# A 512-column up-projection, x in 256-column pieces ahead of its weight rows, and an output over two queues

## The chip, the cores and the metric

The kernel runs on one core of a Trainium2 chip. The metric is device time in microseconds (us) for one execution. A core has TensorE (PE) for matrix products, VectorE (DVE), ScalarE (ACT) and GpSimd (POOL) for elementwise work, and SyncE (SP), which here issues nearly all transfers. PE's weight loads have a row of their own (PEld) in the profile. PSUM, where PE accumulates, has 8 banks of 128 partitions x 512 fp32.

## The reference

`x` is 256 x 2048, fp32, one layer. Cut to what matters:

```
h = rmsnorm(x) * norm_mix_g
z = h @ w_in                      # 2048 x 3072: ssm_in | u | v, 1024 columns each
a = glu(S5(ssm_in))               # 64 groups of a complex state space, then a 1024 x 1024 gate
b = SGU(u, v)                     # causal mixing of positions in chunks of 128
x = x + concat(rmsnorm(a), rmsnorm(b)) @ w_out        # 2048 x 2048
x = x + relu(rmsnorm(x) @ w_up)**2 @ w_down           # 2048 x 8192, 8192 x 2048
y = rmsnorm(x)
```

## The kernel before, in words

**Three products for one.** Every fp32 operand is split into a rounded part (hi) and the rest (lo). A product is then hi·xh + hi·xl + lo·xh, with xh and xl the two parts of the activations. All are added up in one PSUM bank.

**The weight stream.** `wparts` brings the weights through in parts of 512 KB: two 128-row tiles of 512 columns (`raw`, one transfer on SP, L152). `split` makes `whi` on ACT (L105) and `wlo` on DVE (L106). There are three buffers of each and four raw ones. The very first part is "fine": two transfers and two splits, one per 128-row tile.

**Two kinds of block.** `block_A` puts weights into the array and streams activations: for each of four 128-column slices `m` and each row tile it does three matmuls of 256 columns (L186, L187, L188: hi·xh, hi·xl, lo·xh), into `banks[m // 2]`, so two banks hold the four slices. `block_B` keeps activations in the array and streams 512 weight columns (L202 to L204).

**The stages.** In order: w_in for z (block_A on two column blocks, then `z_out`, which scales by the row norm `rsB`), sgu v and u, w_out, glu, the other half of w_out, then four rounds (`NF`) of four block_A on w_up and four block_B on w_down. In w_up the activations are `x2T[:, k, 0]` and `x2T[:, k, 1]` (xh and xl, 256 positions each, neighbours in memory). After a w_up block each bank goes through a relu on ACT, and on DVE the square; ACT then writes its hi part `ht[..., 0]` and DVE the lo part. The S5 work runs in the background as generators that `pump` advances after each part. The last w_down block has a bank of its own kind, `accL` (L1048 to L1050): rows 0 to 127 (t = 0) with 512 columns, rows 128 to 255 (t = 1) with two pieces of 256.

**The start.** SP issues gnat (the norm's weights, 16 x 128), the first 256 columns of x (two row halves, `xin`), the first weight tile, and so on; `hooks` is a list of functions that are called one per weight part and issue further pieces of x (512 columns each) and small parameters. PE first does eight dummy matmuls (`pwarm`, L279), then transposes gnat (`pv`, L283) and x (`ptx`, L297). `prep_x(i)` makes two row tiles of `xT`: ACT writes the hi part times gnat (L300), DVE the lo part (L301). `x_stats` (ACT, squares of x) and `x_rstd` give `rsB`.

**The end.** `last_add` adds the last product to `dacc` (L984), squares it with a sum (ACT, L987) into `ss3`, and multiplies by the final norm's weights. `rstd_sqrt` (L268 to L273) computes the inverse root from the sum of the partial sums (L1054); four pieces of 512 columns per t are scaled (L1059, L1061, L1063) and written by SP (L1064).

**What sets the order.** The program is written as one stream; a scheduler orders instructions on each engine, with a planned time for each, within the limits of data and buffers. `tc.issue_after(ins)` adds a limit: what is issued in it stands behind `ins`. `fence` and `behind` use it to keep small matmuls between large ones. `psa` has four PSUM banks for large products, `psx` one and `pss` three for small ones.

Of the kernel before, what the change touches and what calls it, by code (L numbers as in the profile page):

```python
# [49 lines left out]
def hybrid_layer_kernel(  # L50
# [19 lines left out]
    psx = ctx.enter_context(tc.tile_pool(name="psx", bufs=1, space=PSUM))  # L70
    pss_ = ctx.enter_context(tc.tile_pool(name="pss", bufs=3, space=PSUM))
# [13 lines left out]

    def acc(shape, name="acc"):
        return psa.tile(shape, F32, tag="acc", name=nm(name))
# [16 lines left out]
    def split(hi, lo, src):  # L104
        A.activation(hi, src, AF.Copy)  # L105
        V.tensor_sub(lo, src, hi.bitcast(F32))  # L106
# [34 lines left out]
    hooks = []  # L141

    def wparts(w, k0, nk, c0, places=None):

        wp, kd = stream["pool"], stream["kd"]
        for q in range(0, nk, kd):
            raw = wp.tile([P, kd, 512], F32, tag="raw", bufs=stream["raw"], name=nm("raw"))
            r0_ = (k0 + q) * P
            fine = stream.pop("fine", False)
            step = 1 if fine else kd  # L150
            for s in range(0, kd, step):
                nc.sync.dma_start(  # L152
                    raw[:, s : s + step],
                    w[r0_ + s * P : r0_ + (s + step) * P, c0 : c0 + 512].rearrange("(k p) c -> p k c", p=P),
                )
                if fine and s == 0:
                    hooks.pop(0)()
            if hooks:
                hooks.pop(0)()
            for s in range(0, kd, KS):  # L160
                if places:
                    hi, lo = places[(q + s) // KS]
                else:
                    hi = wp.tile([P, KS, 512], F32R, tag="whi", bufs=3, name=nm("whi"))
                    lo = wp.tile([P, KS, 512], F32R, tag="wlo", bufs=3, name=nm("wlo"))
                if fine:
                    for kk in range(KS):
                        split(hi[:, kk], lo[:, kk], raw[:, s + kk])
                else:
                    split(hi, lo, raw[:, s : s + KS])  # L170
                yield q + s, hi, lo

    def block_A(w, k0, nk, c0, act):


        banks = [acc([P, 2, S], "accA") for _ in range(2)]
        for kp0, hi, lo in wparts(w, k0, nk, c0):
            for m in range(4):
                o = banks[m // 2][:, m % 2]
                ms = slice(m * P, m * P + P)  # L180
                for kk in range(KS):
                    kp = kp0 + kk
                    xh, xl = act(kp)
                    first = kp == 0 and m % 2 == 0
                    with behind():
                        T.matmul(o, hi[:, kk, ms], xh, start=first, stop=False, skip_group_check=True)  # L186
                    T.matmul(o, hi[:, kk, ms], xl, start=False, stop=False, skip_group_check=True)  # L187
                    T.matmul(o, lo[:, kk, ms], xh, start=False, stop=(kp == nk - 1), skip_group_check=True)  # L188
                pump(stream["d"] / 4)
        return banks  # L190
# [25 lines left out]
    def load_x(c, n=512):  # L216
        cs_ = slice(c, c + n)
        for t in range(2):
            nc.sync.dma_start(xin[t][:, cs_], x[t * P : (t + 1) * P, cs_])
# [6 lines left out]
    def load_vecs():  # L226
        r0 = 0
        for v in (norm_mlp_g, ong_ssm, ong_sgu, glu_b):
            n = v.shape[1] // P
            nc.sync.dma_start(vnat[r0 : r0 + n, :], v[0].rearrange("(k p) -> k p", p=P))  # L230
            r0 += n

    nc.sync.dma_start(gnat, norm_mix_g[0].rearrange("(k p) -> k p", p=P))
    load_x(0, 256)


# [27 lines left out]
    def rstd_sqrt(dst, ss, scale, n):  # L264

        m = const.tile([P, n], F32, name=nm("rq_m"))
        t1 = const.tile([P, n], F32, name=nm("rq_t"))
        A.activation(dst, ss, AF.Sqrt, scale=scale, bias=eps_c)  # L268
        V.tensor_scalar(m, ss, scale, EPS, ALU.mult, ALU.add)
# [8 lines left out]
    for i in range(WARMUPS):  # L278
        T.matmul(pwarm, onesm, onesm, start=True, stop=True)  # L279

    def prep_vecs(dst, nat, n):
        pv = aux([P, n], "pv")
        T.transpose(pv, nat, ident[:n, :n])  # L283
        V.tensor_copy(dst, pv)
# [6 lines left out]
    def prep_x(i):  # L291

        pt = acc([P, 2, S], "ptx")
        for kk in range(2):
            k = 2 * i + kk
            for t in range(2):
                T.transpose(pt[:, kk, t * P : (t + 1) * P], xin[t][:, k * P : (k + 1) * P], ident)  # L297
        for kk in range(2):
            k = 2 * i + kk
            xins[i] = A.activation(xT[:, k, 0], pt[:, kk], AF.Copy, scale=g_mix[:, k : k + 1])  # L300
            V.scalar_tensor_tensor(  # L301
                xT[:, k, 1], pt[:, kk], g_mix[:, k : k + 1], xT[:, k, 0].bitcast(F32),
                ALU.mult, ALU.subtract,
            )

    xins = {}

    def x_stats(j):
        with tc.issue_after(xins[2 * j + 1].ins):
# [20 lines left out]
    prep_vecs(vecs[:, 0:16], gnat, 16)  # L330
    prep_x(0)
    hook((load_x, 256, 256))
    hook((load_x, 512), (prep_x, 1))
    hook((load_x, 1024), (prep_x, 2), (prep_x, 3))
    hook((load_x, 1536), (x_stats, 0))
    hook((load_small,), (prep_x, 4), (prep_x, 5))
    hook((x_stats, 1))
    hook((prep_x, 6), (prep_x, 7), (x_stats, 2))
    hook((x_stats, 3), (x_rstd,))
# [69 lines left out]
    def gen_scalars():  # L409

        pa = sx([P, 64], "pa")
        T.transpose(pa, anat, ident[:64, :64])
        V.tensor_copy(lam.rearrange("p a q -> p (a q)"), pa)
        ldt = s32("ldt")
        lv = ldt_all.rearrange("p (q g) -> p q g", g=2)
        for g in range(2):
            V.tensor_copy(ldt[g * 64 : (g + 1) * 64, :], lv[g * 64 : (g + 1) * 64, :, g])
# [50 lines left out]
    def gen_ct():  # L468
# [3 lines left out]
        for i, src in enumerate((b_re, b_im, c_re, c_im)):  # L472
            rows_ = bcn[i * 32 : (i + 1) * 32]
            if i < 2:
                nc.sync.dma_start(rows_, src[0].rearrange("(q g) p h -> q (g p h)", g=2))
            else:
                for g in range(2):
                    nc.sync.dma_start(
                        rows_.rearrange("q (c g p) -> q g c p", c=16, g=2)[:, g],
                        src[0].rearrange("(q g) c p -> q g c p", g=2)[:, g],  # L480
                    )
        for e in range(4):
            nc.sync.dma_start(dnat[:, e, :], ssm_d[0].rearrange("(q g) c -> q (g c)", g=2))
# [3 lines left out]
        for which in range(2):  # L487
            rs_ = slice(which * 64, (which + 1) * 64)
            for h2 in range(2):
                pc = sx([P, 8, 2, 32], "pc")  # L490
                for h8 in range(8):
                    T.transpose(
                        pc[:, h8].rearrange("p i q -> p (i q)"),
                        (bn if which == 0 else cn)[:, h2 * 8 + h8], ident[rs_, rs_],
                    )
# [477 lines left out]
    front.close()  # L973
    mp = ctx.enter_context(tc.tile_pool(name="mlp", bufs=1))
# [6 lines left out]
    def last_add(t, c, cw, bank):  # L981
# [56 lines left out]
    for t in range(2):  # L1038
        ts_ = slice(t * P, t * P + P)
        cw = 512 if t == 0 else 256  # L1040
        for c in range(0, 512, cw):
            bank = acc([P, cw], "accL")
            for kp0, hi, lo in parts:
                for kk in range(KS):
# [5 lines left out]
                    T.matmul(bank, xl[:, ts_], wh, start=False, stop=(kp == 15))  # L1050
            last_add(t, c0 + c, cw, bank)
        s3 = const.tile([P, 1], F32, name=nm("s3"))
        r3 = const.tile([P, 1], F32, name=nm("r3"))
        V.tensor_reduce(s3, ss3[:, t], AX.X, ALU.add)  # L1054
        rstd_sqrt(r3, s3, 1.0 / D, 1)
        for n in range(4):
            ns = slice(n * 512, (n + 1) * 512)
            if n == 0:
                V.tensor_scalar(dacc[:, t, ns], dacc[:, t, ns], r3, None, ALU.mult)  # L1059
            elif n == 3:  # L1060
                V.scalar_tensor_tensor(dacc[:, t, ns], dacc[:, t, ns], r3, gfin[:, ns], ALU.mult, ALU.mult)  # L1061
            else:
                A.activation(dacc[:, t, ns], dacc[:, t, ns], AF.Copy, scale=r3)  # L1063
            nc.sync.dma_start(out[t * P : (t + 1) * P, ns], dacc[:, t, ns])  # L1064
# [29 lines left out]
```

## Time and profile before

| what | value |
|---|---|
| three runs | 1062.08, 1059.5, 1062.22 us, median 1062.08 us |
| the profiled execution | 1060.78 us, span 1059.0 us from first to last instruction |
| granted TensorE clock, mean | 0.994 |
| HBM read and written | 189.91 MB and 4.19 MB, 183 GB/s over the span |
| L186, L187, L188 in w_up | 1024 matmuls each |
| weight splits | 337 on ACT (mean 1058 ns), 337 on DVE (mean 1221 ns) |

A row of a group or of the timeline gives start, length, engine, line, operation and tiles ("out<-in"), the shape of output and input, and in square brackets the idle time before it with what ended it. Matmul lengths reach from issue to the modelled end and overlap; their starts tell the pace. In a table of windows the columns are the stretch, its length, busy time (and instructions) of PE, PEld, DVE, ACT and POOL, the granted clock (1.00 is full), the share of the transfer engines, and GB/s. The waits view gives the engine, tile and line that waited, what it waited for, the total, how often, and the longest.

### The profile page before, as it was taken

What the parts mean: (1) busy time and instruction counts of PE and PEld (TensorE: products, weight loads), DVE (VectorE), ACT (ScalarE), POOL (GpSimd) and SP (SyncE); (2) the same over time, 40 slices, a digit from 0 to 9 for tenths busy, and PEclk for the clock granted to TensorE, in tenths of its full rate; (3) what the DMA queues carried; (4) which work ended last, traced back from release to release, by engine and by line L of the source; (5) the groups of instructions that cost most, each with busy time, mean ns of one, the idle gap of its engine ahead of it and who ended that gap; (6) DMA issues with size and microseconds to landing.
All of it is one profiled execution on the core that took longest, in us unless ns stands there. A gap on an engine that the chain in (4) does not pass through costs nothing.

```text
span 1059.0 us, 16980 instructions
## 1 busy us (share of the span) xinstructions
PE 1043.3 (99%) x6881; PEld 951.1 (90%) x6881; DVE 651.3 (62%) x888; ACT 532.1 (50%) x685; POOL 9.5 (1%) x22
## 2 busy tenths in 40 slices
PE   8999999999999999999999999999999999999996
PEld 7997899978989999888999988899998889998886
DVE  6899988686687555544455555545555565555564
ACT  5668676663766444544444443344444434444453
POOL 0101000000000000000000000000000000000000
PEclk8999999999999999999999999999999999999998
DMA  8774554566565666666666666666666666666662
GB/s 239 225 224 133 141 159 105 155 219 196 181 221 178 180 183 184 191 193 192 192 181 182 187 189 196 198 182 183 184 187 191 191 197 182 184 184 187 195 205 97
DMA packets 112047, 195.25 MB, mean 184 GB/s; under 512 B 17753, under 2 KB 21537, under 8 KB 111521
## 3 DMA queue, kind: packets, MB, share of 16 engines
q1 hardware_dynamic: 111712, 194.13, 61.4%
q8 instruction: 54, 0.88, 0.4%
q14 instruction: 25, 0.20, 0.1%
q0 software_dynamic: 256, 0.03, 0.0%
HBM read 189.91 MB, written 4.19 MB: 183 GB/s over the span
## 4 chain that ended last, share of the span: by engine, by line
PE 90%; ACT 3%; DVE 3%; DMA 2%; issue 1%; SPq 0%; ACTq 0%
PE accA L186 14%; PE accA L188 14%; PE accA L187 14%; PE accB L203 14%; PE accB L204 14%; PE accB L202 14%; PE pf L664 1%; DMA raw<-in_w_in_dram 1%; ACT Tp L631 1%; DMA bcn<-in_ssm_c_im_dram 1%; DVE wlo L106 1%; PE py L704 1%; PE accL L1050 1%; PE accL L1049 1%; PE accL L1048 1%
## 5 line engine op out<-in xcount | busy, mean ns | idle before, releaser
L106 DVE TENSOR_TENSOR wlo<-raw,whi 128x1024 fp32r<-128x1024 f32 (+1 forms) x337 | 411.3, 1221 | 372.1 <-ACT whi L105 371.5
L105 ACT ACTIVATE whi<-raw 128x1024 fp32r<-128x1024 f32 (+1 forms) x337 | 355.9, 1058 | 454.9 <-PE accB L204 200.9
L186 PE MATMUL accA<-x2T,whi 128*128 128x256 f32 x1024 | 289.6, 283 | 0.0
L187 PE MATMUL accA<-x2T,whi 128*128 128x256 f32 x1024 | 289.6, 283 | 0.0
L188 PE MATMUL accA<-x2T,wlo 128*128 128x256 f32 x1024 | 289.2, 283 | 0.0
L187 PEld LDWEIGHTS accA<-x2T,whi 128*128 128x128 f32 x1024 | 196.6, 192 | 0.2
L186 PEld LDWEIGHTS accA<-x2T,whi 128*128 128x128 f32 x1024 | 196.6, 192 | 0.2
L188 PEld LDWEIGHTS accA<-x2T,wlo 128*128 128x128 f32 x1024 | 196.3, 192 | 0.0
L203 PE MATMUL accB<-wlo,hT 128*128 128x512 f32 x480 | 186.8, 389 | 0.0
L204 PE MATMUL accB<-whi,hT 128*128 128x512 f32 x480 | 186.7, 389 | 0.0
L202 PE MATMUL accB<-whi,hT 128*128 128x512 f32 x480 | 168.0, 389 | 0.0
L204 PEld LDWEIGHTS accB<-whi,hT 128*128 128x128 f32 x480 | 90.1, 188 | 18.7
L203 PEld LDWEIGHTS accB<-wlo,hT 128*128 128x128 f32 x480 | 90.1, 188 | 18.5
L202 PEld LDWEIGHTS accB<-whi,hT 128*128 128x128 f32 x480 | 90.1, 188 | 18.6
L186 PE MATMUL accA<-xT,whi 128*128 128x256 f32 x256 | 73.5, 294 | 2.4 <-ACT xT L300 2.4
L187 PE MATMUL accA<-xT,whi 128*128 128x256 f32 x256 | 73.8, 291 | 0.0
L188 PE MATMUL accA<-xT,wlo 128*128 128x256 f32 x256 | 72.5, 290 | 0.0
L186 PEld LDWEIGHTS accA<-xT,whi 128*128 128x128 f32 x256 | 49.3, 195 | 3.3 <-ACT xT L300 2.7
L187 PEld LDWEIGHTS accA<-xT,whi 128*128 128x128 f32 x256 | 50.0, 195 | 0.6 <-DVE xT L301 0.3
L188 PEld LDWEIGHTS accA<-xT,wlo 128*128 128x128 f32 x256 | 49.5, 196 | 0.2
L203 PE MATMUL accB<-wlo,xT 128*128 128x512 f32 x64 | 25.8, 403 | 0.0
L204 PE MATMUL accB<-whi,xT 128*128 128x512 f32 x64 | 25.1, 392 | 0.0
(285 smaller groups left out, 1079.9 us busy)
## 6 DMA issues: line engine op xcount, KB each, us to landing
raw<-in_w_up_dram SPq DMA_DIRECT2D x128, 512.0 KB, 3.7
raw<-in_w_down_dram SPq DMA_DIRECT2D x128, 512.0 KB, 4.0
raw<-in_w_in_dram SPq DMA_DIRECT2D x47, 512.0 KB, 4.2
raw<-in_w_out_dram SPq DMA_DIRECT2D x32, 512.0 KB, 4.7
raw<-in_ssm_glu_w_dram SPq DMA_DIRECT2D x8, 512.0 KB, 4.4
x<-in_x_dram SPq DMA_DIRECT2D x2, 1024.0 KB
out_dram<-dacc SPq DMA_DIRECT2D x8, 256.0 KB, 2.6
xin<-in_x_dram SPq DMA_DIRECT2D x6, 256.0 KB, 7.1
```

The lines of the kernel that those rows point to most:

```text
L105: A.activation(hi, src, AF.Copy)
L106: V.tensor_sub(lo, src, hi.bitcast(F32))
L186: T.matmul(o, hi[:, kk, ms], xh, start=first, stop=False, skip_group_check=True)
L187: T.matmul(o, hi[:, kk, ms], xl, start=False, stop=False, skip_group_check=True)
L188: T.matmul(o, lo[:, kk, ms], xh, start=False, stop=(kp == nk - 1), skip_group_check=True)
L202: T.matmul(banks[t], xh[:, ts_], hi[:, kk], start=(kp == 0), stop=False)
L203: T.matmul(banks[t], xh[:, ts_], lo[:, kk], start=False, stop=False)
L204: T.matmul(banks[t], xl[:, ts_], hi[:, kk], start=False, stop=(kp == nk - 1))
L631: A.activation(Tp[e * 32 : (e + 1) * 32, :, g, 3 - e : 4, :], k4[:, :, 0 : e + 1, :], AF.Copy, scale=gmask[:, g : g + 1],)
L664: T.matmul(pfs[r][i][:, q], w1s[r][:, i, q], u2[r][:, q], start=True, stop=True)
L704: last = T.matmul(py[g * 64 : (g + 1) * 64, q], Gp[:, q, g].rearrange("p j c -> p (j c)"), Eg[:, q, g], start=False, stop=True, skip_group ...
L1048: T.matmul(bank, xh[:, ts_], wh, start=(kp == 0), stop=False)
```

## The change

It has three parts.

1. **w_up.** `block_A2` multiplies hi by xh and xl in one matmul of 512 columns (the two lie side by side) and adds lo·xh with one of 256 columns into the second half of the bank, so that hi·xh stands in columns 0 to 255 and hi·xl + lo·xh in 256 to 511. Each slice `m` has a bank of its own, four per block. The pools `psx` and `pss` are closed after the mixed stage, and their four banks become `psm`, with which `psa` takes turns. After a block, ACT copies the second half of each bank to `cr` and DVE adds the first half.
2. **The start.** x comes in pieces of 256 columns, each ahead of the weight part that it meets; the second row half of the first piece is issued by ACT, gnat by GpSimd. The transposes of piece i are done in the middle of the weight part before it (`mids`). There are twice two more `pwarm` matmuls between the first transposes. In the first part of block 0 the order is `which` (0, 2, 1) outside and `m` inside. `x_stats` and `x_rstd` come after block 0. Some parameter loads are tied behind a weight transfer, and groups of small transposes behind large products.
3. **The end.** The partial sums up to the last piece are added before it, and `rstd_sqrt` takes them as its bias beside the last piece's own sum. The output goes out in four (t = 0) or five (t = 1) pieces over SP's and ACT's queues.

```
@@ pools
+    psx = front.enter_context(tc.tile_pool(name="psx", bufs=1, space=PSUM))
+    pss_ = front.enter_context(tc.tile_pool(name="pss", bufs=3, space=PSUM))
...
+    acc_pools = [psa]
     def acc(shape, name="acc"):
-        return psa.tile(shape, F32, tag="acc", name=nm(name))
+        acc_pools.append(acc_pools.pop(0))
+        return acc_pools[-1].tile(shape, F32, tag="acc", name=nm(name))
@@ the up-projection's block
+    def block_A2(w, k0, nk, c0, act):
+        banks = [acc([P, 2, S], "accA") for _ in range(4)]
         for kp0, hi, lo in wparts(w, k0, nk, c0):
             for m in range(4):
-                o = banks[m // 2][:, m % 2]
+                o = banks[m]
                 ms = slice(m * P, m * P + P)
                 for kk in range(KS):
                     kp = kp0 + kk
-                    xh, xl = act(kp)
...
-                    T.matmul(o, hi[:, kk, ms], xl, start=False, stop=False, skip_group_check=True)
-                    T.matmul(o, lo[:, kk, ms], xh, start=False, stop=(kp == nk - 1), skip_group_check=True)
+                    xhl = act(kp)
+                    T.matmul(o, hi[:, kk, ms], xhl, start=(kp == 0), stop=False, skip_group_check=True)
+                    T.matmul(
+                        o[:, 1], lo[:, kk, ms], xhl[:, 0], start=False, stop=(kp == nk - 1),
+                        skip_group_check=True,
+                    )
@@ w_up
     front.close()
+    psm = ctx.enter_context(tc.tile_pool(name="psm", bufs=4, space=PSUM))
+    acc_pools[:] = [psa] * 4 + [psm] * 4
...
-            banks = block_A(w_up, 0, 16, f * 2048 + cb * 512, act_x2T)
+            banks = block_A2(w_up, 0, 16, f * 2048 + cb * 512, lambda k: x2T[:, k])
...
-                A.activation(rl, banks[i], AF.Relu)
-                V.scalar_tensor_tensor(sq, banks[i], 0.0, rl, ALU.max, ALU.mult)
+                cr = mp.tile([P, 2, S], F32, tag="cr", bufs=2, name=nm("cr"))
+                for mm in range(2):
+                    b_ = banks[i * 2 + mm]
+                    A.activation(cr[:, mm], b_[:, 1], AF.Copy)
+                    V.tensor_tensor(cr[:, mm], b_[:, 0], cr[:, mm], ALU.add)
+                A.activation(rl, cr, AF.Relu)
+                V.scalar_tensor_tensor(sq, cr, 0.0, rl, ALU.max, ALU.mult)
@@ the start
-    nc.sync.dma_start(gnat, norm_mix_g[0].rearrange("(k p) -> k p", p=P))
-    load_x(0, 256)
+    load_x(0, (nc.sync, nc.scalar))
+    nc.gpsimd.dma_start(gnat, norm_mix_g[0].rearrange("(k p) -> k p", p=P))
...
+            if i == 0:
+                with tc.issue_after(tr.ins):
+                    keep_warm(2)
...
+    for i in range(1, 8):
+        hook((load_x, i * 256), *([(load_small,)] if i == 3 else []))
+        mids.append(lambda last, i=i: prep_x(i, last))
...
+        if n == 0:
+            for j in range(4):
+                x_stats(j)
+        with tc.high_priority(offset=0):
+            if n == 0:
+                x_rstd()
@@ the end
-        V.tensor_reduce(s3, ss3[:, t], AX.X, ALU.add)
-        rstd_sqrt(r3, s3, 1.0 / D, 1)
+            if c + cw == 512:
+                s3 = const.tile([P, 1], F32, name=nm("s3"))
+                V.tensor_reduce(s3, ss3[:, t, 0 : (c0 + c) // 256], AX.X, ALU.add)
+                V.tensor_scalar(s3, s3, 1.0 / D, EPS, ALU.mult, ALU.add)
             last_add(t, c0 + c, cw, bank)
+        rstd_sqrt(r3, ss3[:, t, i3 : i3 + 1], 1.0 / D, s3, 1)
+        for a, b, eng, q in (
+            (D - cw, D, None, nc.sync), (512, 1024, A, nc.scalar), (0, 512, V, nc.sync),
+            (1024, D - 512, V, nc.sync), (D - 512, D - cw, A, nc.scalar),
+        ):
```

How the instructions stand on the engines, at three places. PE at the start: `accA` is the product of block 0, `ptx` and `pv` the transposes of x and of gnat, xin_84 and xin_85 the two row halves of x. Before, and then after:

```order
L279 MATMUL pwarm_108<-onesm 128x128 x8
L283 MATMUL pv_121<-ident,gnat 128x16
L297 MATMUL ptx_124<-ident,xin_84 128x128
L297 MATMUL ptx_124<-ident,xin_85 128x128
L297 MATMUL ptx_124<-ident,xin_84 128x128
L297 MATMUL ptx_124<-ident,xin_85 128x128
```

```order
L330 MATMUL pwarm_108<-onesm 128x128 x8
L351 MATMUL ptx_124<-ident,xin_84 128x128 x2
L330 MATMUL pwarm_108<-onesm 128x128 x2
L336 MATMUL pv_121<-ident,gnat 128x16
L351 MATMUL ptx_124<-ident,xin_85 128x128 x2
L330 MATMUL pwarm_108<-onesm 128x128 x2
L194 MATMUL accA_162<-xT,whi_169 128x256 x2
```

After, the transposes of xin_84 stand ahead of gnat's, dummy matmuls stand behind each pair, and only one piece of x is transposed ahead of the first product.

ACT and SP at the start (`raw` is a weight part, `whi` its rounded part, `xT` the transposed x). ACT before, ACT after, SP before, SP after:

```order
L105 ACTIVATE whi_176<-raw_160 128x512 x2
L300 ACTIVATE xT<-ptx_124,vecs 128x256
L300 ACTIVATE xT<-ptx_167,vecs 128x256
L300 ACTIVATE xT<-ptx_124,vecs 128x256
L300 ACTIVATE xT<-ptx_167,vecs 128x256
```

```order
L268 DMA xin_85<-in_x_dram 128x256
L297 ACT_TABLE_LOAD
L297 ACTIVATE warm<-eps_c 128x1
L109 ACTIVATE whi_169<-raw_164 128x512
L357 ACTIVATE xT<-ptx_124,vecs 128x256 x2
L109 ACTIVATE whi_169<-raw_164 128x512
```

```order
L233 DMA gnat<-in_norm_mix_g_dram 16x128
L219 DMA xin_84<-in_x_dram 128x256
L219 DMA xin_85<-in_x_dram 128x256
L152 DMA raw_160<-in_w_in_dram 128x512
L219 DMA xin_84<-in_x_dram 128x256
L219 DMA xin_85<-in_x_dram 128x256
L152 DMA raw_160<-in_w_in_dram 128x512
```

```order
L268 DMA xin_84<-in_x_dram 128x256
L158 DMA raw_164<-in_w_in_dram 128x512 x2
L268 DMA xin_84<-in_x_dram 128x256
L268 DMA xin_85<-in_x_dram 128x256
L158 DMA raw_208<-in_w_in_dram 128x2x512
```

On ACT the copies of x moved from behind both halves of the first split to between them; on SP both halves of the first weight part moved ahead of the second piece of x.

PE in a w_up block (`whi` and `wlo` are one part's halves), before and after:

```order
L186 MATMUL accA_3970<-x2T,whi_4093 128x256
L187 MATMUL accA_3970<-x2T,whi_4093 128x256
L188 MATMUL accA_3970<-x2T,wlo_4094 128x256
L186 MATMUL accA_3970<-x2T,whi_4093 128x256
L187 MATMUL accA_3970<-x2T,whi_4093 128x256
L188 MATMUL accA_3970<-x2T,wlo_4094 128x256
```

```order
L234 MATMUL accA_4135<-x2T,whi_4207 128x512
L235 MATMUL accA_4135<-x2T,wlo_4208 128x256
L234 MATMUL accA_4135<-x2T,whi_4207 128x512
L235 MATMUL accA_4135<-x2T,wlo_4208 128x256
L234 MATMUL accA_4136<-x2T,whi_4207 128x512
L235 MATMUL accA_4136<-x2T,wlo_4208 128x256
```

Three matmuls of 256 columns became one of 512 and one of 256, and the bank changes after two tiles.

More of the change, by code (lines that the diff above doesn't have):

```diff
@@ L167, in wparts @@
                     for kk in range(KS):
-                        split(hi[:, kk], lo[:, kk], raw[:, s + kk])
-                else:
-                    split(hi, lo, raw[:, s : s + KS])
+                        with ExitStack() as order:
+                            for ins in (gmix_in,) if kk == 0 else xins[0]:
+                                order.enter_context(tc.issue_after(ins.ins))
+                            first = split(hi[:, kk], lo[:, kk], raw[:, s + kk])
+                else:
+                    p = q // KS - 1
+                    with ExitStack() as order:
+                        if first:
+                            for ins in (*xins[p], *first):
+                                order.enter_context(tc.issue_after(ins.ins))
+                        split(hi, lo, raw[:, s : s + KS])
                 yield q + s, hi, lo
@@ L176, in block_A, with product @@
         banks = [acc([P, 2, S], "accA") for _ in range(2)]
+        def product(m, kk, which, kp, hi, lo):
+            wt = (hi, hi, lo)[which][:, kk, m * P : m * P + P]
+            return T.matmul(
+                banks[m // 2][:, m % 2], wt, act(kp)[which == 1],
+                start=(kp == 0 and m % 2 == 0 and which == 0), stop=(kp == nk - 1 and which == 2),
+                skip_group_check=True,
+            )
+        for kp0, hi, lo in wparts(w, k0, nk, c0):
+            if kp0 == 0 and len(mids) == 7:
+                for kk in range(KS):
+                    for which in (0, 2, 1):
+                        for m in range(4):
+                            last = product(m, kk, which, kk, hi, lo)
+                    if kk == 0:
+                        mids.pop(0)(last)
+                pump(stream["d"])
+                continue
+            for m in range(4):
+                for kk in range(KS):
+                    for which in range(3):
+                        with behind() if which == 0 else nullcontext():
+                            last = product(m, kk, which, kp0 + kk, hi, lo)
+                stream["last"] = last
+                if m == 1 and mids:
+                    mids.pop(0)(last)
+                pump(stream["d"] / 4)
+        return banks
+    def block_A2(w, k0, nk, c0, act):
+        banks = [acc([P, 2, S], "accA") for _ in range(4)]
         for kp0, hi, lo in wparts(w, k0, nk, c0):
             for m in range(4):
-                o = banks[m // 2][:, m % 2]
+                o = banks[m]
                 ms = slice(m * P, m * P + P)
@@ L182, in block_A @@
                     kp = kp0 + kk
-                    xh, xl = act(kp)
[L184 to L187, printed above, removed]
-                    T.matmul(o, lo[:, kk, ms], xh, start=False, stop=(kp == nk - 1), skip_group_check=True)
-                pump(stream["d"] / 4)
+                    xhl = act(kp)
+                    T.matmul(o, hi[:, kk, ms], xhl, start=(kp == 0), stop=False, skip_group_check=True)
+                    T.matmul(
+                        o[:, 1], lo[:, kk, ms], xhl[:, 0], start=False, stop=(kp == nk - 1),
+                        skip_group_check=True,
+                    )
         return banks
@@ L277, in hybrid_layer_kernel, with keep_warm @@
     pwarm = sx([P, P], "pwarm")
-    for i in range(WARMUPS):
-        T.matmul(pwarm, onesm, onesm, start=True, stop=True)
+    def keep_warm(n):
+        for _ in range(n):
+            T.matmul(pwarm, onesm, onesm, start=True, stop=True)
+    keep_warm(WARMUPS)
     def prep_vecs(dst, nat, n):
@@ L411, in gen_scalars @@
         pa = sx([P, 64], "pa")
[L412 to L413 removed]
         ldt = s32("ldt")
         lv = ldt_all.rearrange("p (q g) -> p q g", g=2)
[L416 to L417 removed]
+        with tc.issue_after(stream["last"].ins), tc.issue_after(xins[3][1].ins):
+            T.transpose(pa, anat, ident[:64, :64])
+            V.tensor_copy(lam.rearrange("p a q -> p (a q)"), pa)
+            for g in range(2):
+                V.tensor_copy(ldt[g * 64 : (g + 1) * 64, :], lv[g * 64 : (g + 1) * 64, :, g])
         dt_, er, th, rad, r4 = t32("dt"), t32("er"), t32("th"), t32("rad"), t32("r4")
@@ L490, in gen_ct @@
                 pc = sx([P, 8, 2, 32], "pc")
[L491 to L495, printed above, removed]
+                with tc.issue_after(stream["last"].ins):
+                    for h8 in range(8):
+                        last = T.transpose(
+                            pc[:, h8].rearrange("p i q -> p (i q)"),
+                            (bn if which == 0 else cn)[:, h2 * 8 + h8], ident[rs_, rs_],
+                        )
+                fence(last)
                 dst = (Bt if which == 0 else Ct)[:, :, :, h2 * 8 : (h2 + 1) * 8]
```

112 lines of the change are left out of this document (55 added, 57 removed).

## The prediction

> **What bounds the kernel now.** I read the page's busy shares and its chain of waits first, because they say which engine's time is worth anything.
>
> ```profile
> PE 1043.3 (99%) x6881; PEld 951.1 (90%) x6881; DVE 651.3 (62%) x888; ACT 532.1 (50%) x685; POOL 9.5 (1%) x22
> PE 90%; ACT 3%; DVE 3%; DMA 2%; issue 1%; SPq 0%; ACTq 0%
> ```
>
> TensorE (PE) is busy 1043.3 of the 1059.0 us span, and 90% of the chain that ended last is its own work. So three things can move the time: the time per matmul, the stretches where PE runs slowly or stands, and the ends. Next I took how matmuls follow each other, since the records of single matmuls overlap and their lengths do not add up. First the timeline of PE in a w_up block (256 columns per matmul), then the chain of waits in a w_down block (512 columns), where each piece starts where the one before ended:
>
> ```profile
> 519.84 0.28 PE L187 MATMUL accA<-x2T,whi 128*128 128x256 f32 x1
> ...
> 522.96 0.28 PE L186 MATMUL accA<-x2T,whi 128*128 128x256 f32 x1
> ```
>
> ```profile
> 460.97 0.23 PE accB L204
> ...
> 463.69 0.23 PE accB L204
> ```
>
> Between the first two rows lie 26 steps in 3.12 us, or 120.0 ns per 256 columns. Between the other two lie 12 matmuls in 2.72 us, or 226.7 ns per 512 columns. The 256 columns more cost 106.7 ns, so 0.4167 ns a column; 256 columns are then 106.7 ns, 512 are 213.3, and each matmul has 13.3 ns on top at either width. That surplus is what fewer matmuls can save.
>
> Then the front: the timeline, and a table of windows for the granted clock (PEclk) and the transfer rate.
>
> ```profile
> 0.80 0.40 SPq L233 DMA_DIRECT2D gnat<-in_norm_mix_g_dram  x1
> 1.11 3.78 PE L279 MATMUL pwarm<-onesm 128*128 128x128 f32 x16 [1.11 <-DVE eps_c L245]
> 5.04 0.73 PE L297 MATMUL ptx<-ident,xin 128*128 128x128 f32 x4
> 5.78 0.63 ACT L105 ACTIVATE whi<-raw 128x512 fp32r<-128x512 f32 x1 [3.48 <-DMA raw<-in_w_in_dram]
> 8.69 0.63 ACT L105 ACTIVATE whi<-raw 128x512 fp32r<-128x512 f32 x1 [2.28 <-DMA raw<-in_w_in_dram]
> 9.22 0.82 ACT L300 ACTIVATE xT<-ptx,vecs 128x256 fp32r<-128x256 f32 x2
> 9.73 0.80 PE L186 MATMUL accA<-xT,whi 128*128 128x256 f32 x2 [2.45 <-ACT xT L300]
> ```
>
> ```profile
> 0.00:8.00 8.00, 5.53 (x25) 4.60 (x25) 4.72 (x11) 2.12 (x3) 1.02 (x8) 1.00 0.54 162
> 8.00:9.00 1.00, 0.00 (x0) 0.00 (x0) 0.00 (x0) 0.31 (x1) 0.00 (x0) 0.82 0.88 274
> 9.00:11.00 2.00, 1.27 (x4) 1.01 (x5) 1.49 (x4) 1.57 (x5) 0.00 (x0) 0.50 1.02 332
> 11.00:14.00 3.00, 3.00 (x16) 3.00 (x15) 1.31 (x3) 2.51 (x6) 0.00 (x0) 0.50 1.02 376
> 15.00:16.00 1.00, 1.00 (x9) 1.00 (x9) 0.00 (x0) 0.00 (x0) 0.00 (x0) 0.77 1.05 369
> 16.00:17.00 1.00, 1.00 (x12) 1.00 (x9) 0.44 (x2) 0.95 (x3) 0.00 (x0) 1.00 1.03 358
> ```
>
> The first product starts only at 9.73. The x columns for it were transposed long before (5.04), but ScalarE (ACT) copied them to SBUF only behind its split of the second weight half, which landed at 8.69 because 256 KB of x lies ahead of it in the queue. PE stood from about 7.3 on; the clock falls to half by 9 (0.82 in 8 to 9 puts the step near 8.7) and comes back in the slice 15 to 16 (0.77, near 15.5 to 15.8). Two costs: a late start, and about 6 us of matmuls at half speed.
>
> **w_up in 512 columns.** Per weight tile three 256-column matmuls (3 × 120.0 = 360.0 ns) become one of 512 and one of 256 (226.7 + 120.0 = 346.7). The sum of columns is the same; one surplus of 13.3 ns goes. 16 blocks × 64 tiles = 1024 such triples: **−13.6 us**. The low end is 0: if the surplus went with the columns after all, nothing is saved; against it stands the 512-column row. I take 13.3, since w_down runs at that width on the same weights' split. The Trainium skill ("TensorE: Matmul & The Clock Gate", section "Wait — 56ns, not 53.3ns?") states a start-to-start time of N ÷ 2.4 GHz plus about 2.5 ns per matmul; by it the term would be 1024 × 2.5 ns = 2.6 us and not 13.6. The trace agrees with its 2.4 GHz (0.4167 ns a column) and not with its 2.5 ns (13.3 here).
>
> The two halves now lie in different columns of a bank, so each block adds four ACT copies and four VectorE (DVE) adds of 128x256 before relu and square. The nearest rows, also 128x256 out of PSUM, in groups by line, and the engines' load in a window:
>
> ```profile
> L300 ACT ACTIVATE xT<-ptx,vecs 128x256 fp32r<-128x256 f32 x16 | 7.0, 468 | 4.6 <-PE ptx L297 4.2 <-DVE xT L301 0.4
> L301 DVE SCALAR_TENSOR_TENSOR xT<-ptx,vecs,xT 128x256 fp32r<-128x256 f32 x16 | 7.4, 479 | 3.4 <-ACT xT L300 3.4
> 500.00:600.00 100.00, 100.00 (x789) 97.95 (x787) 50.23 (x48) 44.53 (x49) 0.00 (x0) 1.00 0.64 186
> 60.00:80.00 20.00, 19.57 (x150) 17.95 (x149) 19.93 (x33) 14.67 (x23) 0.98 (x2) 1.00 0.75 211
> ```
>
> That is 4 × 0.47 + 4 × 0.48 = 3.8 us a block on engines that are busy 45 and 50 of 100 us there. PE goes on meanwhile: a block holds four of the eight banks, and the next has four others. The weight splits queued behind the eviction are covered by three buffers each of whi and wlo, two parts ahead of PE, some 2 × 2.77 us (8 pairs of 346.7 ns a part). Cost 0; with that cover gone 16 × 3.8 = 61 us.
>
> **The front.** The order of first work on PE is now eight pwarm instructions, two transposes of x, two pwarm, gnat's transpose, two transposes, two pwarm, product. The pwarm row ends at 4.89 (16 records are 8 instructions, 0.47 us each), so: 4.89 + 0.2 + 0.94 + 0.1 + 0.2 + 0.94 = 7.3 for the first product, with 0.1 as an estimate for a transpose (four are over in 0.73, the run-out of the last one in it). ACT's copy of x (0.47) lies under the last pwarm pair, and now stands ahead of the second weight half. **−2.4** (9.73 to 7.3). It needs xin_85, now alone on ACT's queue, and the first weight half, which has less ahead of it than the one that started splitting at 5.78.
>
> gnat moves from SP's queue to GpSimd's. The only rows of that queue:
>
> ```profile
> rows<-wbuf POOLq DMA_DIRECT2D x8, 4.0 KB, 3.2
> ```
>
> Issued near 0.8 it lands near 4.0, and PE comes to it at 6.0: 2 us of cover, cost 0; each us beyond that moves the first product. GpSimd has nothing else in a hurry.
>
> **The half clock.** In its place PE has no gap of more than 1 us before the product, so I take the clock as kept: 6.04 us from 9.73 to 15.77 at half speed are 3.0 us of work, **−3.0**. (Zero is the other end.) The Trainium skill ("TensorE: Matmul & The Clock Gate", section "What's actually happening") has the clock halve after an idle window of about 3.4 us and return after one busy window of that length; the fall near 8.7 after PE's transposes fits, the return only some 6 us after the first product is later than that rule gives. Supply is next: each 512 KB part with its 256 KB of x (0.79 MB) lasts 24 products × 0.120 = 2.9 us. By the windows 1.30 MB has landed at 8.0, 1.57 at 9.0, 2.23 at 11.0 and 3.36 at 14.0. The second part (1.57 MB in all) has to have landed at 10.2 less a split of 2.3, so at 7.9, and lands at 9.0: 1 us late, part of it covered since the whi products come before the wlo ones. The fourth (3.15 MB) is due at 13.7 and there at 13.4. **+0.7** (0 to 1.1).
>
> Each x piece's transposes now interrupt block 0, four more of them after the first product than before (4 × 0.1 = **+0.4**). The order of the program shows 90 groups of small matmuls between large ones where it had 70, pw above all (10 groups become 25). What a change of kind costs, from the timeline:
>
> ```profile
> 97.45 1.67 PE L696 MATMUL py<-u,Tp 128*128 128x64 f32 x14
> 98.93 0.48 PE L203 MATMUL accB<-wlo,xT 128*128 128x512 f32 x1
> 99.25 0.40 PE L204 MATMUL accB<-whi,xT 128*128 128x512 f32 x1
> 99.48 0.40 PE L202 MATMUL accB<-whi,xT 128*128 128x512 f32 x1
> ```
>
> The first large matmul behind the group takes 0.32 to the next one's start, which then takes 0.23: 0.1 us a group. 20 × 0.1 = **+2.0** (0 to 2). The extra pwarm are already in the 7.3.
>
> **Waits of the mixed stage.** DVE is full between 60 and 80 us (19.93 of 20) and PE loses little. The waits of PE, by cause:
>
> ```profile
> PE accA L186 <- ACT xT L300: 2.4, 1, 2.4
> PE accB L202 <- ACT whi L105: 1.2, 1, 1.2
> ```
>
> The first is the late start already counted. With x_stats' eight squares taken off ACT until after block 0, and the parameter loads behind weight parts, DVE gets its weights earlier against PE's need from 60 us on; the 1.2 falls into that. Against it: PE starts 5 us earlier in front of the same DVE work, so parts 8 to 10 of the stream (PE reaches them at 31 to 41 us, laying its list end to end), where the strided loads of bcn stand ahead of raw on SP, have less margin. I take **−1.0**, with bounds −3 and +4 (one part's split and load late, 2.3 us, in two places).
>
> **The tail.** From the timeline of the end:
>
> ```profile
> 1050.91 0.42 ACT L987 ACTIVATE junk<-dacc 128x256 f32<-128x256 f32 x1 [5.24 <-DVE dacc L984]
> 1051.45 0.16 DVE L1054 TENSOR_REDUCE s<-ss 128x1 f32<-128x8 f32 x1 [0.64 <-ACT junk L987]
> 1051.65 0.29 ACT L268 ACTIVATE r<-s,eps_c 128x1 f32<-128x1 f32 x1 [0.23 <-DVE s L1054]
> 1053.16 0.75 DVE L1061 SCALAR_TENSOR_TENSOR dacc<-dacc,r,gfin 128x512 f32<-128x512 f32 x1
> 1053.27 1.80 SPq L1064 DMA_DIRECT2D out_dram<-dacc  x4
> ```
>
> The sum over columns (L1054) leaves the chain: 1051.65 − 1051.45 = 0.2. Four issues on one queue (1.80, 0.45 each) become five on two: the last starts about one issue earlier, 0.45. **−0.6** (±0.3).
>
> **Sum:** −13.6 − 2.4 − 3.0 + 0.7 + 0.4 + 2.0 − 1.0 − 0.6 = −17.5 us against the profiled execution's 1060.78 us (span 1059.0 plus 1.8 around it): 1043.3. The median of the three runs is 1062.08, 1.3 above it; I forecast 1043.5.
>
> **Rivals.** (A) The front gives back: PE waits for the second part long enough that the clock halves again, and DVE holds PE at parts 8 to 10. For it speak the 1 us that supply is late and DVE's full windows; against it that 1 us is well under the 2.4 that PE stood. Without the 3.0 of the clock and with the +4 in place of −1.0: 1043.3 + 3.0 to + 8.0, so 1046 to 1051.
> (B) The surplus belongs to the columns, so w_up saves nothing: 1043.3 + 13.6 = 1056.9. Against it stand 120.0 and 226.7; for it only that no row alternates the two widths in one bank. With the skill's 2.5 ns it would be 1054.3.
> (C) The other side: evictions hold PE at each w_up block, because relu waits for cr, cr (two buffers) for the square, and the weight splits for all of it. The price is up to 3.8 a block; over 17.5 ÷ 16 = 1.1 us a block the kernel is slower, at 3.8 it takes 1104. Against it: half-idle engines and four free banks.
> (D) gnat lands so late that the first product is no earlier than 9.73: it must take 2.0 + 2.4 us over 3.2, and then the clock halves too: 1043.3 + 5.4 = 1048.7.
>
> **How the numbers follow.** The forecast's case has 0.68, A 0.19, D 0.04, B 0.05, C 0.04. Around the first, the low end takes the terms' good bounds: supply 0, switches 0, waits −3 (4.7 less, 1038.6); the high end takes in A and D, up to 1051. 1038.5 to 1051 leaves out B, C and edges, less than 2 in 10. This kernel's measurement can't tell 0.3%, 3.2 us, from no change. A, B, D and the forecast are all faster by more; slower is most of C, and no change a part of C: 0.95, 0.02, 0.03.
>
> **What would show it.** In the changed profile: pairs of 346.7 ns in w_up (a 512 row then 120 ns), and three steps' time of 360 if the surplus stays; the first product at 7.3 with PEclk 1.00 in every window up to 16; no wait of PE on ACT's cr copy or DVE's add; the pieces of x no longer ahead of weights in the waits. A wait of PE on wlo or whi between 30 and 65 us over 2 us in sum, or PEclk 0.50 anywhere, would make the forecast too low; the order's 20 more groups costing nothing would make it too high.

## The result, and the profile after

The changed kernel takes 1053.29 us (median of 4 runs, 1052.08 to 1054.66) against 1061.68 us (median of 4): a ratio of 0.9925, 95% interval 0.9904 to 0.9946. It is faster, by 8.4 us and not by 18, and outside the forecast range. The profiled execution took 1054.34 us, with a span of 1052.6; two of the others took 1052.08 and 1052.24. The page's first rows after:

```profile
PE 1036.8 (98%) x5865; PEld 897.0 (85%) x5865; DVE 672.9 (64%) x957; ACT 554.5 (53%) x750; POOL 9.0 (1%) x23
PEclk9999999989999999999999999999999999999998
```

PE is still the bound. But the clock row has an 8 in the ninth slice (210 to 237 us), which the forecast did not have. Now the three places of the prediction. The start, in the timeline, and its windows:

```profile
6.74 0.47 ACT L357 ACTIVATE xT<-ptx,vecs 128x256 fp32r<-128x256 f32 x1 [1.63 <-PE ptx L351]
7.27 0.74 PE L194 MATMUL accA<-xT,whi 128*128 128x256 f32 x4
...
11.56 0.39 PE L194 MATMUL accA<-xT,whi 128*128 128x256 f32 x1 [0.48 <-DVE xT L358]
```

```profile
8.00:9.00 1.00, 1.00 (x11) 1.00 (x10) 0.69 (x2) 0.96 (x3) 0.00 (x0) 1.00 1.05 394
9.00:11.00 2.00, 2.00 (x18) 1.87 (x16) 1.59 (x2) 1.22 (x2) 0.00 (x0) 1.00 0.93 278
11.00:14.00 3.00, 2.50 (x19) 2.22 (x19) 1.99 (x4) 1.42 (x2) 0.00 (x0) 1.00 0.81 265
```

The first product starts at 7.27 (forecast 7.3), and the clock stays at 1.00 where it had been 0.50. A w_up block in round 2, then in round 3 (timeline of PE):

```profile
539.83 0.39 PE L234 MATMUL accA<-x2T,whi 128*128 128x512 f32 x1
540.06 0.27 PE L235 MATMUL accA<-x2T,wlo 128*128 128x256 f32 x1
...
542.95 0.40 PE L234 MATMUL accA<-x2T,whi 128*128 128x512 f32 x1
```

```profile
714.65 0.40 PE L234 MATMUL accA<-x2T,whi 128*128 128x512 f32 x1
...
716.42 0.40 PE L234 MATMUL accA<-x2T,whi 128*128 128x512 f32 x1
```

Nine pairs in 3.12 us are 346.7 ns each, as forecast; in round 3 five pairs take 1.77 us, 354 ns each. The end:

```profile
1043.90 0.28 PE L1118 MATMUL accL<-wlast,hT 128*128 128x256 f32 x1
1045.27 0.29 ACT L318 ACTIVATE r<-ss,s 128x1 f32<-128x1 f32 x1
1046.89 1.30 SPq L1142 DMA_DIRECT2D out_dram<-dacc  x3
```

From the last product's start to the end of the span it is 8.7 us, where it was 9.0.

So each part works, and yet the first product of w_up (x2T) comes later than before. Rows of PE's timeline, before and after:

```profile
331.73 0.28 PE L186 MATMUL accA<-x2T,whi 128*128 128x256 f32 x1
```

```profile
337.24 0.62 PE L234 MATMUL accA<-x2T,whi 128*128 128x512 f32 x2
```

To find where, I took the start of every large matmul in both traces and compared them at equal progress (after minus before): first product −2.46 us; end of block 0, −6.02 (37.58 against 43.60, of which 3.45 are small transposes that now come after the block); 16 products before the end of w_in, −0.13 (206.97 against 207.10); first x2T product, +5.51; last product of all, −6.12. The largest step, 5.6 us, lies within 20 us after the end of w_in. The waits view names it, and the windows show what it set off:

```profile
PE accB L251 <- DVE uT L900: 2.2, 2, 1.6
PE accB L251 <- DVE zst L702: 1.4, 1, 1.4
PE accB L253 <- DVE hl L938: 0.9, 1, 0.9
```

```profile
207.40:210.80 3.40, 3.40 (x25) 2.90 (x24) 3.40 (x5) 1.46 (x2) 0.00 (x0) 1.00 0.74 211
210.80:214.25 3.45, 1.30 (x6) 0.70 (x6) 3.45 (x8) 2.93 (x7) 0.00 (x0) 1.00 0.76 251
214.25:217.70 3.45, 2.51 (x5) 1.60 (x6) 3.40 (x6) 3.39 (x6) 0.00 (x0) 0.50 1.00 344
217.70:221.10 3.40, 3.40 (x14) 3.01 (x14) 3.31 (x7) 3.13 (x6) 0.00 (x0) 0.50 0.72 261
221.10:224.50 3.40, 3.40 (x13) 3.01 (x13) 2.40 (x4) 0.86 (x1) 0.00 (x0) 0.50 0.06 20
```

PE is busy for only 1.30 of 3.45 us while it waits for DVE's eviction of the last w_in banks (uT) and for hl; then the clock is 0.50 for 10.24 us. DVE was late because ACT was. ACT's timeline before, then after, then what DVE made of it before and after:

```profile
194.12 0.72 ACT L584 ACTIVATE cosT<-cosT,halfpi 128x512 f32<-128x512 f32 x1
194.87 1.28 ACT L711 ACT_TABLE_LOAD   x1
196.16 0.60 ACT L711 ACTIVATE yst<-py 128x512 f32<-128x512 f32 x1
```

```profile
197.63 0.60 ACT L769 ACTIVATE yst<-py 128x512 f32<-128x512 f32 x1
...
200.62 1.28 ACT L642 ACT_TABLE_LOAD   x1
201.92 0.72 ACT L642 ACTIVATE cosT<-cosT,halfpi 128x512 f32<-128x512 f32 x1
```

```profile
200.59 0.69 DVE L518 TENSOR_TENSOR tmp<-cosT,pf 128x512 f32<-128x512 f32 x1 [0.19 <-PE pf L664]
...
209.10 0.67 DVE L836 TENSOR_TENSOR uT<-accA,rsB 128x512 f32<-128x512 f32 x1
```

```profile
202.67 0.69 DVE L576 TENSOR_TENSOR tmp<-cosT,pf 128x512 f32<-128x512 f32 x1 [0.81 <-ACT cosT L642]
...
208.75 2.32 DVE L731 TENSOR_TENSOR_SCAN hc<-rhoT,hc 128x512 f32<-128x512 f32 x2
211.18 0.67 DVE L900 TENSOR_TENSOR uT<-accA,rsB 128x512 f32<-128x512 f32 x1
```

Before, the sine that ends cosT stood ahead of yst's gelu on ACT. After, the scheduler put it behind yst and behind a weight split, so ACT loads a function table once more (1.28 us), cosT ends at 202.64, DVE's rotation starts 2.1 us later than before (202.67 against 200.59), and the uT eviction behind the scans with it (211.18 against 209.10).

### The profile page after: what moved, and what is told of

Read it like the earlier page. It is cut to its first block, busy times and chain, and to the rows that moved or that the text cites. A ratio compares the mean times of both kernels' runs of the same rounds, so it can differ in the third digit from the quotient of the medians.

```text
span 1052.6 us, 15093 instructions
## 1 busy us (share of the span) xinstructions
PE 1036.8 (98%) x5865; PEld 897.0 (85%) x5865; DVE 672.9 (64%) x957; ACT 554.5 (53%) x750; POOL 9.0 (1%) x23
## 3 DMA queue, kind: packets, MB, share of 16 engines
HBM read 189.91 MB, written 4.19 MB: 184 GB/s over the span
## 4 chain that ended last, share of the span: by engine, by line
PE 90%; DVE 4%; ACT 2%; issue 1%; DMA 1%; SPq 1%; DVEq 0%
PE accA L234 23%; PE accB L253 14%; PE accB L251 14%; PE accB L252 14%; PE accA L235 11%; PE accA L194 7%; DVE wlo L109 2%; PE pf L722 1%; PE py L754 1%; PE py L762 1%; PE accL L1118 1%; PE accL L1117 1%; PE accL L1116 1%; ACT whi L109 1%; DMA raw<-in_w_in_dram 1%
## 5 line engine op out<-in xcount | busy, mean ns | idle before, releaser
L234 PE MATMUL accA<-x2T,whi 128*128 128x512 f32 x1024 | 355.4, 395 | 0.0
L235 PE MATMUL accA<-x2T,wlo 128*128 128x256 f32 x1024 | 280.3, 278 | 0.0
L234 PEld LDWEIGHTS accA<-x2T,whi 128*128 128x128 f32 x1024 | 191.6, 188 | 43.6
L235 PEld LDWEIGHTS accA<-x2T,wlo 128*128 128x128 f32 x1024 | 192.6, 188 | 1.8
L194 PE MATMUL accA<-xT,whi 128*128 128x256 f32 x512 | 100.3, 292 | 1.0 <-DVE xT L358 0.8
L194 PEld LDWEIGHTS accA<-xT,whi 128*128 128x128 f32 x512 | 80.1, 190 | 4.0 <-DVE xT L358 2.3
L1070 ACT ACTIVATE cr<-accA 128x256 f32<-128x256 f32 x64 | 24.0, 375 | 7.9 <-PE accA L235 7.9
L251 PE MATMUL accB<-whi,hl 128*128 128x512 f32 x64 | 24.6, 412 | 2.2 <-DVE uT L900 2.2
L253 PE MATMUL accB<-whi,hl 128*128 128x512 f32 x64 | 25.3, 409 | 0.9 <-DVE hl L938 0.9
L252 PE MATMUL accB<-wlo,hl 128*128 128x512 f32 x64 | 25.8, 406 | 0.0
```

Source lines behind the costliest of these rows:

```text
L194: return T.matmul(banks[m // 2][:, m % 2], wt, act(kp)[which == 1], start=(kp == 0 and m % 2 == 0 and which == 0), stop=(kp == nk - 1 and ...
L234: T.matmul(o, hi[:, kk, ms], xhl, start=(kp == 0), stop=False, skip_group_check=True)
L235: T.matmul(o[:, 1], lo[:, kk, ms], xhl[:, 0], start=False, stop=(kp == nk - 1), skip_group_check=True,)
L251: T.matmul(banks[t], xh[:, ts_], hi[:, kk], start=(kp == 0), stop=False)
L252: T.matmul(banks[t], xh[:, ts_], lo[:, kk], start=False, stop=False)
L253: T.matmul(banks[t], xl[:, ts_], hi[:, kk], start=False, stop=(kp == nk - 1))
```

## The experiments

**Theory 1:** the late cosT and the half clock behind PE's idle time make the 5.6 us. **Rival:** cosT is a symptom; DVE, or the order of background work, uses up any lead. Kernels that were measured together share their runs of the kernel before, whose median was 1061.8 us for cos_first, keep_busy, late_start and up_only, 1063.05 for cos_busy, front_tail and f_perm, and 1060.47 for ht4; the ratios allow for that. Two more figures help below. One is the stretch from 16 products before the end of w_in to the first x2T product in each profiled execution: 124.6 us before and 130.3 in the changed kernel. The other is the mean granted clock of each run. In the profiled executions it was 0.998 or 0.997 where the clock was halved only behind the last product (cos_busy, ht4), 0.996 with one halved stretch of 3.41 us more (cos_first), 0.994 or 0.995 with two (keep_busy, f_perm) and 0.993 with three (the changed kernel).

**cos_first** (changed kernel):

```
+    cos_in = {}
...
-        A.activation(cosT, cosT, AF.Sin, scale=-6.2831850, bias=halfpi)
+        cos_in[r] = A.activation(cosT, cosT, AF.Sin, scale=-6.2831850, bias=halfpi)
...
-        A.activation(yst, py, AF.Gelu_apprx_tanh)
+        with tc.issue_after(cos_in[r + 1].ins) if r == 2 and r + 1 in cos_in else nullcontext():
+            A.activation(yst, py, AF.Gelu_apprx_tanh)
```

> The changed kernel with one order fixed on ACT: the sine that makes cosT of the last S5 quarter stands ahead of the gelu of yst, as in the kernel before (one function table less is loaded). Theory 1 (this late cosT holds DVE, then PE from 211 to 217 us, and the idle PE halves the clock until 224.5): cosT ends near 195 and not 202.6, no half clock near 214, first x2T product about 5.6 us earlier (331.6), time 1053.3 - 5.6 = 1047.7 us. Rival (DVE is full there for other reasons, or PE's lead was used up before): the first x2T product moves by less than 1.5 us, time 1052 to 1053.5.

Measured: 1049.11 us (ratio 0.9874, 0.9856 to 0.9893). The order of PE, DVE and SP is that of the changed kernel; only ACT's differs, here alone. The first x2T product starts at 332.81, 4.4 us earlier, and the stretch ahead of it takes 125.9 us and not 130.3. Theory 1 holds, though cosT ends at 199.2 and not at 195, and in the profiled execution the clock was still halved for one stretch. ACT, DVE and PE, and then the windows:

```profile
198.49 0.71 ACT L644 ACTIVATE cosT<-cosT,halfpi 128x512 f32<-128x512 f32 x1
...
208.94 0.67 DVE L903 TENSOR_TENSOR uT<-accA,rsB 128x512 f32<-128x512 f32 x1
...
332.81 0.39 PE L234 MATMUL accA<-x2T,whi 128*128 128x512 f32 x1
```

```profile
211.40:214.80 3.40, 1.74 (x7) 0.85 (x6) 3.39 (x6) 3.33 (x7) 0.00 (x0) 1.00 1.00 383
214.80:218.20 3.40, 3.40 (x15) 3.02 (x13) 3.27 (x7) 3.38 (x7) 0.00 (x0) 0.50 1.00 410
218.20:221.60 3.40, 3.40 (x20) 2.95 (x20) 3.40 (x6) 2.19 (x5) 0.00 (x0) 1.00 0.40 154
```

The other three runs had a mean clock of 0.998, so in them it was not halved there.

**keep_busy** (changed kernel): behind the last `pm` matmul

```
-                T.matmul(
+                last_pm = T.matmul(
...
+    pdum = aux([P, P], "pdum")
+    with tc.issue_after(last_pm.ins):
+        for _ in range(6):
+            last_pd = T.matmul(pdum, onesm, onesm, start=True, stop=True)
+    fence(last_pd)
```

> The changed kernel with six dummy matmuls (0.47 us each, 2.8 us in all) on PE between the last sgu matmul (pm) and the first w_out product, where PE stands. Theory 1: the waits stay but the clock is not halved; the dummies take the place of 2 of the 3.1 us of idle, and the half clock's 2.5 to 4.5 us go: 1049 to 1051 us, granted clock 1.00 from 214 to 225. Rival (the clock halves for something else than PE's idleness, or the half clock costs nothing since DVE holds PE anyway): 1053 to 1054.5 us.

Measured: 1050.63 us (ratio 0.9897, 0.9882 to 0.9913), 2.7 less than the changed kernel for doing more work, though the two intervals overlap. Its profiled execution was its slowest (1053.08): there the clock was halved from 216.6 to 223.4, 6.83 us and not 10.24. Its runs show the worth of the clock by themselves: three with a mean clock of 0.998 took 1050.31 to 1050.63 us, one with 0.996 took 1051.6, and this one with 0.994 took 1053.08. The changed kernel's four runs had 0.993 or 0.995. So the dummies helped, but did not keep the clock in every run. Six of them took 1.50 us here and not 2.8. The stretch ahead of the half clock, and the one before it:

```profile
209.77:213.18 3.41, 2.71 (x19) 2.14 (x19) 3.41 (x7) 2.58 (x7) 0.00 (x0) 1.00 0.79 273
213.18:216.60 3.42, 1.66 (x6) 1.09 (x7) 3.41 (x6) 3.37 (x6) 0.00 (x0) 1.00 1.00 410
```

**cos_busy**: cos_first with four dummies at that place.

> The changed kernel with cosT ahead of yst as in cos_first and, besides, four dummy matmuls (1.9 us) on PE behind the last sgu matmul, as in keep_busy. In cos_first the clock was still halved for one stretch of 3.41 us (214.8 to 218.2) behind a stretch in which PE was busy for 1.74 of 3.40 us. If idleness over such a stretch decides, 1.9 us more of work there keeps the clock: no half clock between 205 and 230, and 1049.1 - 1.5 = about 1047.5 us. If the dummies only delay (the waits on DVE are not idle time that can be filled), 1049 to 1051 us.

Measured: 1048.08 us (1047.64 to 1048.61; ratio 0.9864, 0.9848 to 0.988), the lowest here; it beats both kernels. Against cos_first the gain of 1.0 is not clear of noise: the intervals overlap, and cos_first's three runs at 0.998 took 1048.0 to 1049.2. Windows of the same place, with edges that lie a multiple of 3.41 us behind the first clock record of that execution (4.65):

```profile
209.44:212.85 3.41, 3.01 (x20) 2.24 (x18) 3.41 (x6) 3.36 (x9) 0.00 (x0) 1.00 0.97 364
212.85:216.26 3.41, 2.77 (x16) 2.17 (x17) 3.33 (x8) 3.36 (x7) 0.00 (x0) 1.00 1.01 413
```

With 3.01 and 2.77 us of work in the two stretches the clock stays. The first x2T product starts at 330.82, 2.0 us earlier than in cos_first; 0.8 of that is the start, since the first product stood at 6.60 and not at 7.43. No half clock is left before the tail, and the stretch ahead of x2T takes 124.6 us, as before: the whole 5.6 us is back.

**late_start** (changed kernel): `keep_warm(WARMUPS + 10)`.

> The changed kernel with ten more dummy matmuls ahead of the first product, so that it starts 4.7 us later (near 12 us). If DVE and the order of the background work hold the stretch from 40 to 205 us (theory 2: an early start is used up there), the time moves by less than 1.5 us. If PE's own work bounds that stretch, it moves by 4.7 us: 1058 us.

Measured: 1055.09 us (ratio 0.9936, 0.9922 to 0.9951). The ten dummies did not cost what was planned:

```profile
1.11 5.70 PE L330 MATMUL pwarm<-onesm 128*128 128x128 f32 x36 [1.11 <-DVE eps_c L295]
...
8.57 0.73 PE L194 MATMUL accA<-xT,whi 128*128 128x256 f32 x4
```

The first product is 1.30 us later. The end of block 0 is 1.15 later, the end of w_in 1.12 and the first x2T product 1.33. The delay is small, and the scheduler also changed some of PE's order at the start and behind w_in, but it arrives whole: nothing between 40 and 205 us absorbs it. For a delay of this size the rival falls; the 4.7 us that were planned were not tried.

**up_only**: the kernel before with block_A2, its pools and its evictions.

> The kernel before with the 512-column up-projection, its PSUM pools and its evictions alone; front and tail as before. By the prediction's term 13.6 us less than before: 1048 us. By what the changed kernel's trace shows from the first x2T product to the last (11.6 us, one of the four rounds saving only 1.8): 1050 us. Either is faster than the changed kernel, if the front's part loses 5.5 us by the first x2T product as the traces say. If the front gains after all: over 1053.3 us.

Measured: 1051.2 us (1047.87 to 1052.12; ratio 0.9893, 0.9875 to 0.991), so w_up alone has a lower median than the changed kernel, with intervals that overlap. Between the first x2T product and the last product its trace has 706.66 us, as the changed kernel's (706.66), against 718.3 before: −11.6. Its profiled run had a second half clock in the old front:

```profile
25.94:29.35 3.41, 2.36 (x17) 1.95 (x16) 1.24 (x8) 0.77 (x2) 0.00 (x0) 1.00 1.11 198
29.30:36.20 6.90, 6.90 (x34) 6.49 (x35) 3.31 (x13) 3.45 (x9) 0.00 (x0) 0.51 0.80 214
```

The order up to there is that of the kernel before, which in its own trace kept the clock. Whether a stretch of waits halves the clock can thus differ from one execution to the next. Four of the five runs had a mean clock of 0.992 or 0.993 and took 1050.83 to 1052.12 us; the fifth had 0.996 and took 1047.87.

**front_tail**: the changed kernel with the old up-projection.

> The changed kernel with the old up-projection (three 256-column matmuls and the old eviction): front and tail alone. If the parts add up, 1053.3 + 11.6 = 1064.9 us, slower than the kernel before by about 3 us (front +3.4 by the end of the mixed stage in this trace: 5.5 less the half clock that may fall elsewhere; tail -0.3). The prediction's terms for front and tail, -3.9 us, would give 1057.9 us.

Measured: 1066.09 us (1064.65 to 1066.43; ratio 1.003, 1.0019 to 1.0042): front and tail alone made the kernel slower, by 3.0 us against its own runs of the kernel before. With the 10.6 us that up_only gains against its own that makes 7.6 of the 8.4 us measured: the parts add up to within 1 us.

**f_perm**: `w_up` columns and `w_down` rows taken in the order (0, 2, 1, 3)[f].

> The changed kernel with the second and third quarter of the hidden columns exchanged (w_up's columns and w_down's rows), so that the same instructions meet other weights. In the changed kernel the pairs of w_up take 346.7 ns in rounds 1, 2 and 4, and 353.5 ns in round 3. If the slower pace belongs to the weights' values or their place in HBM, it moves to round 2; if it belongs to the place in the program (instructions, buffers), it stays in round 3. The time is that of the changed kernel either way.

Measured: 1052.3 us (one run); round 3 is still the slow one (0.2365 + 0.117 us a pair, against 0.232 + 0.115 in the other rounds). So it is not the weights.

**ht4**: cos_busy with `bufs=4` for hT.

> cos_busy with four hT tiles and not six, so that each round of w_up and w_down uses the same four; the order on every engine is that of cos_busy. If the slower pairs of round 3 (353.5 ns against 346.7) come from which hT tiles that round uses (with six, round 3 alone has tiles 3 to 6), all rounds have one pace: 346.7 ns and 1048.1 - 1.75 = 1046.3 us, or 353.5 everywhere and 1053 us. If they come from the place in the program, round 3 stays slow: 1048.1 us.

Measured: 1048.47 us (ratio 0.9878, 0.9862 to 0.9894); round 3 is still slow, so it is not the hT tiles either. What makes it slow stays open.

## Why the prediction was wrong

It was right on the sign and wrong on the size. The step that failed is the mixed stage: the prediction took its waits at −1.0 and looked for trouble at 31 to 41 and at 60 to 80 us, and had no term for the change from w_in to w_out, where the runs showed +5.6. That is half of the 11.1 us by which the sum misses the two traces (−17.5 against −6.4). By its terms, from the two traces; where no run is named, none isolates the term:

- **First product, −2.4:** −2.46, in part by luck. The last dummies took 0.45 us and not 0.94, and the product waited for ACT's copy of x (6.74 to 7.21), which was to lie under them; in the traces with this order it starts anywhere from 6.60 to 7.57.
- **Half clock at the start, −3.0:** gone as said, in all eight traces with the new front. In the trace of before, the first 24 products took 2.7 us more than at 0.120 each. The prediction called the return of the clock late; it came behind the first stretch of 3.41 us in which PE was busy throughout (12.05 to 15.46).
- **Supply +0.7 and transposes +0.4:** 2.6. The steps behind the products of block 0 exceed 0.120 us by 4.4 us in sum; before it was 1.8 outside the half clock. PE's idle time in this is 0.9 us (0.1 before). The largest excess is 0.64 at 10.8; most are 0.1 to 0.2, two or more in each weight part, around the transposes. The prediction had counted the pieces' landing, not the chain of transposes, ACT and DVE that now stands inside each part.
- **Switches, +2.0:** 2.4 from block 1 to the end of w_in, beside the 3.45 of transposes that moved behind block 0. PE's order has 68 groups of small matmuls there and had 44; at 0.1 us a group that is 2.4.
- **Waits of the mixed stage, −1.0:** 0 up to the end of w_in. Idle time of PE there is 2.2 us before and after; the 1.2 wait for whi went, and 1.4 for zst came.
- **Not in the sum, +5.6:** the cosT order, the wait for uT and hl, and 10.24 us at half clock, in a place that the prediction did not compare in the two orders. Rival A had the mechanism (DVE holds PE, the clock halves) in the wrong place, and its 1046 to 1051 us were too low as well. In the stretch up to x2T cos_first takes back 4.3 us and cos_busy all 5.6; the medians fall by 4.2 and 5.2.
- **w_up, −13.6:** −11.6. The size per pair was exact in rounds 1, 2 and 4; round 3 gave 1.8 us where the others gave some 3.3. The surplus does go with matmuls, so rival B fell, and the 2.5 ns of the Trainium skill ("TensorE: Matmul & The Clock Gate", section "Wait — 56ns, not 53.3ns?") with it: 13.3 here.
- **Evictions, 0:** right. No wait of PE names them, and they were cheaper than taken:

```profile
L1070 ACT ACTIVATE cr<-accA 128x256 f32<-128x256 f32 x64 | 24.0, 375 | 7.9 <-PE accA L235 7.9
L1071 DVE TENSOR_TENSOR cr<-accA,cr 128x256 f32<-128x256 f32 x64 | 23.9, 415 | 0.0
```

- **Tail, −0.6:** −0.3. **gnat, 0:** right; its transpose started at 6.10.

Sum of what was found: −2.5 − 2.7 + 2.6 + 2.4 + 0 + 5.6 − 11.6 − 0.3 = −6.5, against a span that went from 1059.0 to 1052.6. The medians lie 8.4 apart and not 6.4, in part since the changed kernel's profiled execution was one of its two longer ones.

## What to carry to other kernels

When a scheduler reorders the whole program, compare the order of the other engines, too, at each place where PE waits for an eviction: look for activation functions that moved across one that needs another table. Compare two traces at equal progress of the bounding engine, and a loss that no edit explains stands out at once. Where a short wait of PE can't be removed, a few dummy matmuls in it can pay, since the idle stretch costs twice: once as a wait, and again as half clock.

## What the hardware showed unexpectedly

- The clock goes by fixed stretches of 3.41 us: half clock lasted 3.41, 6.83 or 10.24 us, and every change lies a multiple of 3.41 us behind the first clock record of its execution. PE need not stand for a whole stretch. In the ten traces every stretch at full clock in which PE was busy for less than 1.7 us was followed by half clock, and every one with more than 2.4 us by full clock. In between both occur: the clock fell after 1.75 (cos_first), 2.00 (f_perm) and 2.36 us (up_only, at 25.9), and stayed after 2.17 (before, at 90.6), 2.37 (ht4, at 211.8) and in these two (up_only, then front_tail):

```profile
94.20:97.61 3.41, 1.94 (x14) 1.33 (x13) 2.69 (x4) 3.41 (x6) 0.00 (x0) 1.00 0.00 0
1053.80:1057.21 3.41, 1.75 (x15) 1.54 (x13) 0.90 (x4) 0.80 (x3) 0.00 (x0) 1.00 0.00 0
```

So PE's busy time alone does not decide, and what else counts stays open. Nor is the return fixed: it came behind the first stretch in which PE was busy throughout in cos_first and f_perm, and behind the second in the changed kernel, keep_busy, late_start and front_tail. The Trainium skill ("TensorE: Matmul & The Clock Gate", section "What's actually happening") has the clock fall after at least one idle window of some 3.4 us; the length agrees, but here the stretch was only partly idle. Its remark that the window runs on its own agrees, too: the first record stands at 4.11 to 6.96 us from execution to execution, so the same waits may fall into one stretch or into two. That fits the spread between executions of one kernel, though no run sets the phase.
- Pairs of a 512- and a 256-column matmul can run at 346.7 or at 354 ns, for a whole round, in the same order of instructions; three matmuls of 256 columns took 120.0 ns each in every round.
- The dummy matmuls at the start follow each other by 0.21 us per record up to the first clock record and by 0.11 behind it. In late_start, whose first record stands at 4.11, the last step of 0.21 begins at 3.84 and the steps of 0.11 begin at 4.19. So PE ran at half pace until then, though the profile shows 1.00 there. It also moves the first product: with that record at 4.65 (cos_busy), 5.19 (f_perm), 6.04 (changed kernel) and 6.96 us (ht4) the product started at 6.60, 6.86, 7.27 and 7.57. And it is part of why ten more dummies cost late_start 1.30 us and not 4.7.
